# Two-layer S5/attention trunk on one core: S5 constants in portions, no unread products, and a re-ordered first mixer with feature-major queries and keys

## The chip, the core and the metric

The kernel runs on 1 core of a Trainium2 chip. TensorE (PE in the profile, PEld its weight loads), VectorE (DVE), ScalarE (ACT), GpSimd (POOL) and SyncE (SP, which here only issues DMAs) have queues of their own; 16 DMA engines move data. A matmul loads a stationary operand of up to 128 columns and streams the moving operand past it into a PSUM bank. The metric is device time in microseconds; each version is run several times and the median counts.

## What is computed

A trunk of two layers over 256 tokens of 1024 features, float32 in and out. Each layer is half a SwiGLU FFN, a mixer, half a SwiGLU FFN, all with residuals; the first mixer joins an S5 state space model with multi-head latent attention:

```python
def _even_mixer(h, ...):
    u, c_q, c_kv, k_rope = split(h @ w_in, [512, 896, 1152])
    s5_out = _s5(u, ...)                       # diagonal complex states, GELU, gated by a 512x512 product
    q  = rmsnorm(c_q)  @ w_uq                  # 8 heads, 64 plain + 32 rotary
    kv = rmsnorm(c_kv) @ w_ukv                 # 8 heads, 64 key + 64 value
    q_pe, k_pe = rope(q[..., 64:]), rope(k_rope)   # k_pe is shared by the heads
    o = causal_attention([q_nope, q_pe], [k_nope, k_pe], v)
    return concat([s5_out, o]) @ w_out
def reference(x, ...):
    for l in (0, 1):
        x += 0.5 * swiglu(rmsnorm(x)); x += mixer_l(rmsnorm(x)); x += 0.5 * swiglu(rmsnorm(x))
    return rmsnorm(x)
```

The S5 recurrence runs over blocks of four tokens. Powers of the state matrix, the input matrices and the matrices inside a block depend on the weights alone and are made on the chip.

## The kernel before, in words

The tokens are two tiles of 128. Every weight chunk comes by one or two DMAs of 512 KB on SP's queue into one of five stage buffers (`Weights.load`), and `Weights.pre` splits it into a high half (a cast to fp32r by ACT, line 71) and the rest (a subtraction by DVE, line 72). Products with weights are then three fp32r products: high x high, rest x high, high x rest. Transposes, scores, attention values and the S5 products are plain fp32, two passes each except the transposes. The framework orders each engine's queue from the program's order and from its own forecast of when operands are ready; `tc.issue_after(i)` keeps instructions of a block behind instruction `i` on the engine of `i`.

`ffn` loops over 22 blocks of 128 hidden features (`gate_up`, `down`). `begin` norms the residual and makes it feature-major; for the first FFN it also starts the loads and issues 13 small products (`going`, line 262) whose results nothing reads. The first FFN carries `setup()` as a background: after each block, `aside` takes steps of this generator until a budget of 2400 (elements plus 140 for each DVE instruction) is spent; `pause` ends a call at once. `setup` is the rotary tables, a few constants, then `s5_prep`.

`mixer0` runs in this order: the products for cq, ckv, u (`product`, line 771), token-major; `latents` (normed cq and ckv, feature-major); `queries(0)`; u into blocks of four tokens; `keys_values(0)`; `block_inputs` of both halves of the 16 state pairs; `heads_turned`, which transposes queries and keys of each head on PE; then `attend(h)` for eight heads with scores two heads ahead, and between them `states` (DVE multiplications and two scans; half of the read-out on POOL), `outputs` (48 fp32 passes for each half, lines 1030 to 1032), `gelu`, and `glu`; last the output product. `rope` on the queries and the key runs on POOL. At the very end `finish` norms the rows and writes them out.

Of the kernel before, what the change touches and what calls it, by code (L numbers as in the profile page):

```python
# [29 lines left out]
class Weights:  # L30
# [8 lines left out]
    def plan(self, specs):  # L39

        self.specs = list(specs)
        self.pieces = [(i, c) for i, s in enumerate(self.specs) if s is not None
                       for c in range(0, s[0].shape[1], 1024)]

    def load(self, n):
        for i, c in self.pieces[self.loaded:self.loaded + n]:
            ap = self.specs[i][0]
            w = min(1024, ap.shape[1] - c)
# [5 lines left out]
    def pre_in_pieces(self):  # L54
# [14 lines left out]
        for c in range(0, ap.shape[1], 1024):  # L69
            t, w = self.raw.pop(0)  # L70
            nc.scalar.copy(out=hi[:, c:c + w], in_=t[:, :w])  # L71
            nc.vector.tensor_tensor(out=lo[:, c:c + w], in0=t[:, :w], in1=hi[:, c:c + w].bitcast(F32),  # L72
                                    op=ALU.subtract)
            self.load(1)
            yield
# [19 lines left out]
def trunk(ctx: ExitStack, tc: tile.TileContext, x, pos, invf, wff, gains, w_u, w_cq, w_ckv,  # L95
# [72 lines left out]
    def ffn_specs(j):  # L168
# [5 lines left out]
    mix0 = [(w, True) for w in (w_cq[0], w_cq[1], w_ckv[0], w_ckv[1], w_u[0], w_u[1], w_uq[0], w_ukv[0], w_uq[1],  # L174
                                w_ukv[1], w_out0[2], w_glu, w_out0[3], w_out0[0], w_out0[1])]
# [7 lines left out]

    def rsqrt(out, a):

        nc.gpsimd.tensor_tensor(out=out, in0=a, in1=mhalf[:, :a.shape[1]], op=ALU.pow)  # L186
# [48 lines left out]

    def aside(background, quota, last):
# [9 lines left out]
    def begin(prev, row):  # L246
# [5 lines left out]
        if acc is None:  # L252
# [4 lines left out]

            idle = bank("idle")

            def going(n):  # L260
                for _ in range(n):
                    nc.tensor.matmul(idle[:, :128], ident, ident, start=True, stop=True)

            going(4)
# [7 lines left out]
            W.load(STAGED - 2)  # L272
# [6 lines left out]
        if acc is None:  # L279
            pieces = W.pre_in_pieces()  # L280
            ups.append(next(pieces))
            with tc.issue_after(last):
                next(pieces)
            turned_0 = transpose_split(y0, KT, yh, yl, 0)
            going(3)
            with behind_both(turned_0):
                next(pieces)
                r1 = residual(1, acc, factor)
# [5 lines left out]
        y1, last = normed(1, *r1, g)  # L294
# [133 lines left out]
    def sincos(ang, cos, sin, n, tmp):  # L428

        k, kh, r = tmp("k", n), tmp("kh", n), tmp("r", n)  # L430
# [12 lines left out]
        ts(r, r, 3.1415925, -3.1415925, ALU.min, ALU.max)  # L443
        nc.scalar.activation(out=sin, in_=r, func=AF.Sin)
        nc.scalar.activation(out=cos, in_=r, func=AF.Sin, scale=0.5)
        tt(cos, cos, cos, MUL)
# [19 lines left out]

    def cmul_halves(ore, oim, ar, ai, br, bi, t1, t2):
# [13 lines left out]
    ss1 = cst.tile([128, 2, 16], F32, name="ss1")  # L481

# [35 lines left out]
    def rope_tables():  # L518
# [6 lines left out]
        sincos(ang, co, si, 48, lambda n, m: small("rt" + n, m))  # L525
        for t in range(2):
            for (cc, ss, o, h) in ((cc0, ss0, 0, 16), (cc1, ss1, 16, 8)):
# [5 lines left out]
                nc.vector.tensor_copy(out=ss[:, t, h:], in_=s)  # L533

# [29 lines left out]
    def s5_prep():  # L564
# [7 lines left out]
        sc = cst.tile([128, 20, NPAIR], F32, name="s5sc")  # L572
        slots = iter(range(20))
# [17 lines left out]
        dt, mag, ang, co, si = new(), new(), new(), new(), new()  # L591
# [8 lines left out]
        tt(ang, li, dt, MUL)  # L600
        yield
        exp_finish(mag, w, t1, c)
        yield
        sincos(ang, co, si, n, tmp)
        yield

# [4 lines left out]
        cmul(ar[2], ai[2], ar[1], ai[1], ar[1], ai[1], t1, t2)  # L611
        yield
        cmul(ar[3], ai[3], ar[2], ai[2], ar[1], ai[1], t1, t2)
        cmul(ar[4], ai[4], ar[2], ai[2], ar[2], ai[2], t1, t2)
# [10 lines left out]
        cmul(dr, di, co, si, co, si, t1, t2)  # L625
        yield
        er, ei = new(), new()
        cmul(er, ei, dr, di, dr, di, t1, t2)
# [7 lines left out]
        while m < NBLK:  # L636
            nr, ni = (dr, di) if m in (2, 8, 32) else (er, ei)
            orr, oi = (er, ei) if m in (2, 8, 32) else (dr, di)
            cmul(nr, ni, orr, oi, orr, oi, t1, t2)
# [75 lines left out]
        def pause():  # L715
            spent[0] += 1 << 20
            yield

# [5 lines left out]
        yield from pause()  # L724
        for q0 in range(0, NPAIR, 4):
# [745 lines left out]
```

## Time and profile before

| | us |
|---|---|
| median of three runs | 1036.1 |
| the runs | 1036.10, 1028.13, 1036.48 |
| the profiled execution, its span | 1032.36, 1030.5 |
| PE busy | 1003.2 (97%) |
| DVE, ACT, POOL busy | 669.9, 569.1, 50.4 |

Mean granted clock of TensorE over the span: 0.987; 1.00 is 2.4 GHz, 0.50 is 1.2 GHz. An engine's busy time says when instructions of it run; a wait is counted on the engine that stands still and put down to what ended it. A row of the timeline gives start, duration, engine, line, what is written from what, shape and count; merged rows give the time from the first start to the last end.

### The profile page before, as it was taken

The numbers are of one execution on the slowest core, as the hardware profiler recorded it, in microseconds if no ns is written. First come the engines' busy times: TensorE is split into PE (matmuls) and PEld (weight loads), VectorE is DVE, ScalarE is ACT, GpSimd is POOL, SyncE is SP. The second block draws the span as 40 slices with busy tenths as digits, with TensorE's granted clock in tenths as the row PEclk, the third lists the DMA queues.
The fourth block names the chain that finished last, engine by engine and source line by source line (L and its number), as shares of the span: only waits on it lengthen the run. The fifth ranks groups of instructions, "written<-read, shape, count | busy, mean of one in ns | idle before, by whom it ended". The sixth has DMA issues, their size and how long they took to land.

```text
span 1030.5 us, 14762 instructions
## 1 busy us (share of the span) xinstructions
PE 1003.2 (97%) x5540; PEld 861.3 (84%) x5540; DVE 669.9 (65%) x1245; ACT 569.1 (55%) x1030; POOL 50.4 (5%) x81
## 2 busy tenths in 40 slices
PE   8999999989889999999999999999999999999997
PEld 7788899878788888888888888888878887888885
DVE  4889874565867776555558555554657777655543
ACT  5555663666536665555446555553567756555543
POOL 3010000002510000000000000000001100000000
PEclk9999999999969999999999999999999999999999
DMA  8856554316113586555618556553453548656621
GB/s 259 273 153 209 187 187 144 123 46 199 53 42 124 199 291 193 192 188 189 212 56 292 186 191 186 188 192 128 162 165 123 147 137 288 189 192 192 187 80 41
DMA packets 49801, 174.80 MB, mean 170 GB/s; under 512 B 6081, under 2 KB 7105, under 8 KB 49730
## 3 DMA queue, kind: packets, MB, share of 16 engines
q1 hardware_dynamic: 48576, 170.20, 51.0%
q10 hardware_dynamic: 1154, 3.67, 1.1%
q8 instruction: 43, 0.70, 0.3%
q14 instruction: 28, 0.23, 0.1%
HBM read 172.80 MB, written 1.05 MB: 169 GB/s over the span
## 4 chain that ended last, share of the span: by engine, by line
PE 80%; DVE 7%; ACT 4%; DMA 4%; issue 3%; POOL 1%; SPq 0%; POOLq 0%; ACTq 0%; DVEq 0%
PE gu L322 24%; PE acc L355 22%; PE gu L324 12%; PE proj L771 6%; DMA stage<-in_wff_dram 3%; PE acc L782 3%; PE gu L338 2%; DVE wlo L72 2%; PE pu L771 1%; ACT whi L71 1%; PE gt L375 1%; DMA lam<-in_s_lam_dram 1%; PE pt L206 1%; PE ckv L771 1%; PE pz L1063 1%
## 5 line engine op out<-in xcount | busy, mean ns | idle before, releaser
L322 PE MATMUL gu<-y,whi 128*128 128x512 f32 x1216 | 432.6, 398 | 0.0
L72 DVE TENSOR_TENSOR wlo<-stage,whi 128x1024 fp32r<-128x1024 f32 (+1 forms) x236 | 281.2, 1201 | 178.8 <-ACT whi L71 178.5
L324 PE MATMUL gu<-y,wlo 128*128 128x256 f32 x1216 | 341.2, 281 | 0.0
L71 ACT CAST whi<-stage 128x1024 fp32r<-128x1024 f32 (+1 forms) x236 | 240.6, 1033 | 106.7 <-PE gu L322 72.6
L322 PEld LDWEIGHTS gu<-y,whi 128*128 128x128 f32 x1216 | 228.5, 188 | 55.4
L324 PEld LDWEIGHTS gu<-y,wlo 128*128 128x128 f32 x1216 | 229.6, 189 | 2.6
L355 PE MATMUL acc<-dhi,hs 128*128 128x512 f32 x704 | 195.6, 396 | 6.0 <-ACT hs L143 4.6
L355 PEld LDWEIGHTS acc<-dhi,hs 128*128 128x128 f32 x704 | 127.6, 190 | 35.2 <-ACT hs L143 6.0
L72 DVE TENSOR_TENSOR dlo<-stage,dhi 128x1024 fp32r<-128x1024 f32 x88 | 107.1, 1218 | 37.6 <-ACT dhi L71 37.6
L71 ACT CAST dhi<-stage 128x1024 fp32r<-128x1024 f32 x88 | 92.2, 1049 | 44.4 <-DMA stage<-in_wff_dram 44.4
L355 PE MATMUL acc<-dlo,hs 128*128 128x512 f32 x352 | 111.7, 393 | 0.0
L132 DVE TENSOR_TENSOR both<-gu,both 128x256 f32<-128x256 f32 x152 | 63.8, 420 | 55.7 <-ACT both L325 55.4
L325 ACT COPY both<-gu 128x256 f32<-128x256 f32 x152 | 56.0, 369 | 75.8 <-PE gu L324 75.7
L355 PEld LDWEIGHTS acc<-dlo,hs 128*128 128x128 f32 x352 | 67.0, 190 | 14.7
L143 ACT CAST hs<-sh 128x256 fp32r<-128x256 f32 x80 | 32.5, 407 | 71.1 <-DVE sh L132 71.0
L771 PE MATMUL proj<-whi,y 128*128 128x512 f32 x192 | 62.5, 396 | 0.2 <-ACT y L143 0.2
L328 ACT ACTIVATE sh<-both 128x256 f32<-128x256 f32 x76 | 31.8, 419 | 41.7 <-DVE both L132 41.5
L375 PE MATMUL gt<-whi,y 128*128 128x256 f32 x256 | 49.7, 288 | 0.8 <-ACT y L143 0.7
L771 PEld LDWEIGHTS proj<-whi,y 128*128 128x128 f32 x192 | 36.1, 188 | 8.3 <-ACT y L143 0.5
L375 PEld LDWEIGHTS gt<-whi,y 128*128 128x128 f32 x256 | 40.8, 191 | 2.2 <-ACT y L143 2.2
L186 POOL TENSOR_TENSOR rs<-rs,mhalf 128x1 f32<-128x1 f32 x14 | 7.7, 552 | 670.0 <-DVE rs L140 670.0
L132 DVE TENSOR_TENSOR hs<-sh,hs 128x256 fp32r<-128x256 f32 x80 | 33.4, 418 | 7.9 <-ACT hs L143 7.9
(324 smaller groups left out, 1107.1 us busy)
## 6 DMA issues: line engine op xcount, KB each, us to landing
stage<-in_wff_dram SPq DMA_DIRECT2D x264, 512.0 KB, 4.6
stage<-in_w_in_dram SPq DMA_DIRECT2D x24, 512.0 KB, 4.5
stage<-in_w_out_dram SPq DMA_DIRECT2D x16, 512.0 KB, 3.6
gain<-in_gains_dram ACTq DMA_DIRECT2D x6, 512.0 KB, 5.7
stage<-in_w_u_dram SPq DMA_DIRECT2D x4, 512.0 KB, 4.2
xr<-in_x_dram SPq DMA_DIRECT2D x2, 512.0 KB, 5.2
stage<-in_w_cq_dram SPq DMA_DIRECT2D x2, 512.0 KB, 3.8
stage<-in_w_ckv_dram SPq DMA_DIRECT2D x2, 512.0 KB, 4.9
```

Of the source, the lines that this page charges most:

```text
L71: nc.scalar.copy(out=hi[:, c:c + w], in_=t[:, :w])
L72: nc.vector.tensor_tensor(out=lo[:, c:c + w], in0=t[:, :w], in1=hi[:, c:c + w].bitcast(F32), op=ALU.subtract)
L132: return nc.vector.tensor_tensor(out=out, in0=a, in1=b, op=op)
L143: copy = nc.scalar.copy(out=hi, in_=src)
L322: nc.tensor.matmul(gu, gh[:, k, s, :], y2[:, k].rearrange("p s c -> p (s c)"), start=k == 0, stop=False)
L324: nc.tensor.matmul(gu[:, :SEQ], gl[:, k, s, :], yh[:, k, :], start=False, stop=k == KT - 1)
L325: nc.scalar.copy(out=both[:, s], in_=gu[:, SEQ:])
L328: nc.scalar.activation(out=sh[:, 0, :], in_=both[:, 0], func=AF.Silu)
L355: nc.tensor.matmul(acc[t][c], a[:, sl], w[:, c * 512:(c + 1) * 512], start=(f == 0 and n == 0), stop=(f == NF - 1 and n == 2))
L375: last = nc.tensor.matmul(o, a[:, k, sl], w[:, k * 256:(k + 1) * 256], start=(k0 == 0 and n == 0), stop=(k0 > 0 and n == 11))
L771: last = nc.tensor.matmul(acc, a[:, k0 + k, sl], w[:, k * width:(k + 1) * width], start=(k0 == 0 and n == 0), stop=(k0 + per == nk and n = ...
L782: mm = nc.tensor.matmul(acc[t][c], a[:, k0 + k, sl], w[:, o:o + 512], start=(first and k == 0 and n == 0), stop=(last and k == 1 and n == 2))
```

## The change

Early part and first FFN. The 13 unread products go; the second input tile is loaded after one weight piece, not after two. `setup` takes its three generators side by side in three portions, one for each of the first three blocks, behind the last root on POOL (`last_root`), and then runs the rest. Complex squares are made with four instructions in place of six (`csquare`). Every second copy in `within` goes from ACT to DVE.

First mixer. u is projected first, then cq and ckv. Queries and keys are made feature-major directly, with the weights as the stationary operand: each head has 128 rows, 64 plain, 32 rotary and 32 swapped rotary, so that a product with a table (`qtab`) from PSUM does the rotation and the scores' contraction adds both parts; the weight chunk for queries is loaded in pieces of 768 columns and widened from 96 to 128 columns a head while it is split. The shared key part is rotated once on POOL, transposed and copied to all heads. The S5 states are a generator of five steps, all on DVE, taken between other work. Scores run three heads ahead, a head's probabilities are transposed one head ahead, and the first output product is put between heads. `gelu` copies its PSUM bank out first. In `finish` the gain is multiplied in by quarters, and the two scalings and writes are 640 and 384 columns wide.

```diff
 class Weights:
+    def step(spec):
+        return 768 if spec[1] == "queries" else 1024
...
+            if wide == "queries":
+                rows = slice(c // 96, (c + w) // 96)
+                h, l = (a[:, :1536].rearrange("p (r d) -> p r d", d=128)[:, rows] for a in (hi, lo))
+                v = t[:, :w].rearrange("p (r d) -> p r d", d=96)
+                parts = [(h[:, :, :96], l[:, :, :96], v)]
+                parts += [(h[:, :, a:a + 16], l[:, :, a:a + 16], v[:, :, b:b + 16]) for a, b in ((96, 80), (112, 64))]
+            for h, l, v in parts:
+                nc.scalar.copy(out=h, in_=v)
+                nc.vector.tensor_tensor(out=l, in0=v, in1=h.bitcast(F32), op=ALU.subtract)
...
 def begin(prev, row):
-            going(4)
...
-            going(6)
             nc.sync.dma_start(out=xr[0], in_=x[:128])
-            W.load(2)
+            W.load(1)
             nc.sync.dma_start(out=xr[1], in_=x[128:])
...
-            going(3)
...
-        y1, last = normed(1, *r1, g)
+        with behind_both(turned_0):
+            y1, last = normed(1, *r1, g)
...
 def mixer0(prev):
+        cq, ckv = ([bank(n)[:, :w] for _ in range(2)] for n, w in (("cq", 384), ("ckv", 288)))
+        project(cq, 0, 384)
+        u_blocks()
+        project(cq, 1, 384)
+        cqy = [low_rank(cq[t], 384, qg[:, :384]) for t in range(2)]
+        project(ckv, 0, 288)
+        st.append(states(0, *block_inputs(0)))
+        step(0)
+        project(ckv, 1, 288)
+        cky = [low_rank(ckv[t][:, :256], 256, qg[:, 384:]) for t in range(2)]
+        kd = key_rotation()
...
+        step(0)
+        st.append(states(1, *block_inputs(1)))
...
 def queries(g):
+            for b in range(2):
+                pq = bank("pq").rearrange("p (h c) -> p h c", h=2)
+                for j in range(2):
+                    for n, (k, w, a) in enumerate(highs_first(range(3), wh, wl, cqh, cql)):
+                        nc.tensor.matmul(pq[:, j], w[:, k, 2 * b + j], a[:, k, :], start=n == 0, stop=n == 8)
+                h = 4 * g + 2 * b
+                tt(qT[:, h:h + 2, :], pq, qtab.unsqueeze(1).to_broadcast([128, 2, SEQ]), MUL)
...
 def states(b, v_re, v_im):
+            for z, x, y, op in ((z_re, v_re, v_im, ADD), (z_im, v_im, v_re, SUB)):
+                tt(z, x, c, MUL)
+                tt(t1, y, s, MUL)
+                tt(z, z, t1, op)
+                yield
             scan(z_re)
             scan(z_im)
             yield
...
-            for out, x, y, op in ((xs_im[:, h, o], z_re[:, :, a], s[:, :, a], MUL), (t2, z_im[:, :, a], c[:, :, a], MUL),
-                                  (xs_im[:, h, o], xs_im[:, h, o], t2, ADD)):
-                nc.gpsimd.tensor_tensor(out=out, in0=x, in1=y, op=op)
+            for xs, x, y, op in ((xs_re, z_re, z_im, SUB), (xs_im, z_im, z_re, ADD)):
+                tt(xs[:, h, o], x[:, :, a], c[:, :, a], MUL)
+                tt(t1, y[:, :, a], s[:, :, a], MUL)
+                tt(xs[:, h, o], xs[:, h, o], t1, op)
+                yield
...
+        queries(0)
...
+        step(1)
+        keys(0)
+        step(0)
+        key_values(0)
+        for h in range(3):
+            sc[h] = scores(h)
+        step(1)
+        step(0)
         queries(1)
+        step(0)
+        sc[0] = turned(sc[0], pb)
         attend(0)
+        step(1)
+        keys(1)
+        key_values(1)
         attend(1)
+        step(1)
         yp = outputs(0)
         attend(2)
+        step(1)
         attend(3)
         osb = normalised(0)
+        g0 = gelu(yp)
         yp = outputs(1)
         heads_out(0, osb)
+        attend(4)
...
 def setup():
-        rope_tables()
-        yield from mixer_constants()
-        yield from s5_prep()
+        parts = [mixer_constants(), s5_prep(), rope_tables()]
+        for _ in range(3):
+            with tc.issue_after(last_root[0]):
+                for part in parts:
+                    next(part, None)
+            yield from pause()
+        for part in parts[:0:-1]:
+            yield from part
```

## Rows read from the trace of the kernel before

**Rows 1.** Windows: stretch, length, busy of PE, PEld, DVE, ACT, POOL; PEclk, DMA, GB/s.

```profile
0.00:12.10 12.10, 10.64 (x39) 7.87 (x39) 3.43 (x6) 4.64 (x8) 5.48 (x16) 1.00 0.85 310
12.10:48.60 36.50, 32.59 (x200) 28.46 (x199) 28.18 (x51) 23.42 (x35) 3.43 (x2) 0.95 0.82 253
48.60:210.70 162.10, 162.10 (x953) 142.35 (x951) 119.01 (x288) 94.95 (x159) 6.54 (x5) 1.00 0.53 165
210.70:220.60 9.90, 7.23 (x25) 5.50 (x25) 5.99 (x11) 4.32 (x11) 0.56 (x1) 0.83 0.26 96
220.60:344.50 123.90, 115.23 (x686) 103.39 (x687) 87.65 (x172) 64.84 (x145) 23.88 (x40) 0.93 0.32 108
281.00:287.00 6.00, 0.59 (x4) 0.46 (x4) 6.00 (x9) 0.03 (x1) 3.66 (x3) 0.79 0.00 0
287.00:301.30 14.30, 14.30 (x65) 13.83 (x66) 8.25 (x18) 3.94 (x8) 0.77 (x1) 0.50 0.24 74
```

**Rows 2.** Waits of PE: line, cause: total us, times, longest us.

```profile
PE yp L1031 <- DVE xs_re L132: 5.4, 1, 5.4
PE acc L355 <- ACT hs L143: 4.6, 3, 2.3
PE pt L206 <- DVE y L136: 2.5, 5, 1.2
PE po L1003 <- ACT pT L804: 1.5, 2, 0.9
```

**Rows 3.** Timeline of the start: start us, us, engine, line, operation.

```profile
6.60 1.43 DVE L136 SCALAR_TENSOR_TENSOR y<-xr,rs,g 128x512 f32<-128x512 f32 x2 [0.74 <-POOL rs L186]
...
7.17 2.93 PE L262 MATMUL idle<-ident 128*128 128x128 f32 x12
...
9.90 1.77 PE L206 MATMUL pt<-ident,y 128*128 128x128 f32 x8
...
11.51 0.83 PE L262 MATMUL idle<-ident 128*128 128x128 f32 x6
...
13.08 2.91 POOL L453 TENSOR_TENSOR s5w<-euler,lam 128x16 f32<-128x16 f32 x1 [4.65 <-DMA lam<-in_s_lam_dram]
...
17.34 0.66 PE L206 MATMUL pt<-ident,y 128*128 128x128 f32 x4 [1.20 <-DVE y L136]
```

**Rows 4.** Timeline of PE, rows of equal products, on the high clock.

```profile
223.44 1.03 PE L771 MATMUL cq<-whi,y 128*128 128x384 f32 x5
...
242.79 1.07 PE L771 MATMUL pu<-whi,y 128*128 128x512 f32 x4
...
250.60 0.34 PE L771 MATMUL pq<-whi,cqh 128*128 128x384 f32 x1
...
261.81 0.61 PE L926 MATMUL v_im<-u,e_im 128*128 128x64 f32 x4
...
265.36 0.60 PE L974 MATMUL pt<-ident,q_sb 128*96 128x128 f32 x4
...
346.84 0.76 PE L375 MATMUL gt<-whi,y 128*128 128x256 f32 x5
```

**Rows 5.** Timeline of PE in outputs(0), on the low clock.

```profile
287.63 0.64 PE L1030 MATMUL yp<-u,tmat 128*128 128x64 f32 x2
```

**Rows 6.** Groups, DVE, 220.6 to 344.5: count | busy us, mean ns | idle before.

```profile
L72 DVE TENSOR_TENSOR wlo<-stage,whi 128x1024 fp32r<-128x1024 f32 x22 | 26.3, 1219 | 8.8 <-ACT whi L71 8.8
...
L937 DVE TENSOR_TENSOR_SCAN z_im<-mag,z_im 128x512 f32<-128x512 f32 x2 | 3.4, 1698 | 0.0
L789 DVE CUSTOM_DVE_ANT_0 s<-sp,mask 128x256 f32<-128x256 f32 x8 | 3.3, 414 | 0.0
...
L937 DVE TENSOR_TENSOR_SCAN z_re<-mag,z_re 128x512 f32<-128x512 f32 x2 | 2.4, 1211 | 0.0
...
L132 DVE TENSOR_TENSOR z_re<-v_re,cosn 128x512 f32<-128x512 f32 x2 | 1.4, 684 | 2.9 <-PE v_re L925 2.9
```

**Rows 7.** Tile xs_re: count, duration min/median/max ns, first and last start.

```profile
L132 DVE TENSOR_TENSOR xs_re<-xs_re,t x2: 668/1180/1691, 285.0 to 291.2; 128x504 f32<-128x504 f32 x2
```

**Rows 8.** Timeline of DVE in the last norm.

```profile
1024.61 0.69 DVE L132 TENSOR_TENSOR yo<-xr,gain 128x512 f32<-128x512 f32 x1
```

More of the change, by code (lines that the diff above doesn't have):

```diff
@@ L533, in rope_tables, with rotation_table @@
                 nc.vector.tensor_copy(out=ss[:, t, h:], in_=s)
+        nc.gpsimd.memset(ct[:, :, :64], 1.0)
+        nc.vector.tensor_copy(out=ct[:, :, 64:96], in_=cc0)
+        nc.vector.tensor_copy(out=ct[:, :, 96:], in_=ss0)
+    def rotation_table():
+        pt = bank("pt")[:, :SEQ]
+        for t in range(2):
+            nc.tensor.transpose(pt[:, t * 128:(t + 1) * 128], ct[:, t], ident)
+        nc.scalar.copy(out=qtab, in_=pt)
     def rope(v, nh, cc, ss, half, eng=None):
@@ L773, in product, with out_product @@
         return last.ins
-    def out_product(acc, t, ws, hi, lo, k0, first, last):
+    def out_product(acc, t, ws, hi, lo, k0, first, last, ks=(0, 1)):
         wh, wl = ws
         sl = slice(t * 128, (t + 1) * 128)
-        for k in range(2):
+        for k in ks:
             for n, (w, a) in enumerate(three(wh, wl, hi, lo)):
@@ new lines, in queries, with keys @@
+            for b in range(2):
[5 more added lines that the diff above has]
+                tt(qT[:, h:h + 2, :], pq, qtab.unsqueeze(1).to_broadcast([128, 2, SEQ]), MUL)
+            more()
+        def keys(g):
+            wh, wl = (w[:, :1024].rearrange("p (k s c) -> p k s c", k=2, s=2) for w in queue[0])
+            pk = bank("pk").rearrange("p (j c) -> p j c", j=2)
+            for j in range(2):
+                for n, (k, w, a) in enumerate(highs_first(range(2), wh, wl, ckh, ckl)):
+                    nc.tensor.matmul(pk[:, j], w[:, k, 0, 128 * j:128 * j + 128], a[:, k, :], start=n == 0,
+                                     stop=n == 5)
+            for r in range(2):
+                nc.scalar.copy(out=kT[:64, 4 * g + r:4 * g + 4:2, :], in_=pk[64 * r:64 * r + 64])
@@ new lines, in key_values @@
+        def key_values(g):
+            wh, wl = (w[:, :1024].rearrange("p (k s c) -> p k s c", k=2, s=2) for w in queue.pop(0))
+            pv = bank("pv").rearrange("p (t c) -> p t c", t=2)
+            for t in range(2):
+                sl = slice(t * 128, (t + 1) * 128)
+                for n, (k, w, a) in enumerate(highs_first(range(2), wh, wl, ckh, ckl)):
+                    nc.tensor.matmul(pv[:, t], a[:, k, sl], w[:, k, 1, :], start=n == 0, stop=n == 5)
+            nc.scalar.copy(out=v_sb[:, :, 256 * g:256 * g + 256], in_=pv)
+            more()
@@ L994, in scores, with values @@
             return s
[L996 removed]
+        def values(h, pT):
             g, k = divmod(h, 4)
@@ L1082, in attend @@
             values(h, sc.pop(h))
-        heads_turned(0)
-        sc = {0: scores(0), 1: scores(1)}
-        next(st[0])
+        queries(0)
+        pt = bank("pt")[:, :SEQ]
+        for t in range(2):
+            nc.tensor.transpose(pt[:, t * 128:(t + 1) * 128], kd[:, t], ident)
+        for g in range(2):
+            nc.scalar.copy(out=kT[64:, 4 * g:4 * g + 4, :], in_=pt[64:].unsqueeze(1).to_broadcast([64, 4, SEQ]))
+        step(1)
+        keys(0)
+        step(0)
+        key_values(0)
```

306 lines of the change are left out of this document (137 added, 169 removed).

## The prediction

> **What bounds the kernel now.** I read the busy time by stages first. From 48.6 to 210.7 us TensorE (PE) is busy all the time at full granted clock [rows 1], so there a shorter VectorE (DVE) or ScalarE (ACT) step is worth nothing; the reader should look for the stages where PE is not full. There are three, and the change touches each. The start (0 to 48.6) has 1.5 + 3.9 us without PE work. The end of the first FFN (210.7 to 220.6) has 2.7 us idle and a mean clock of 0.83. The first mixer (220.6 to 344.5) has 123.9 - 115.2 = 8.7 us idle, and its stretch from 287.0 to 301.3 ran at granted clock 0.50, the 1.2 GHz level, all through: 14.3 / 2 = 7.15 us lost. Next the waits of PE by cause [rows 2]: the longest, 5.4 us, is that of `outputs(0)` for `xs_re`, the S5 states, which DVE makes; in the six microseconds around it DVE is busy 6.00 of 6.00 and PE 0.59 [rows 1]. The clock fell in that wait and came back only after the 48 small products of `outputs(0)` and some of the attention. So the mixer's chain is DVE's S5 states, then a cold PE.
>
> **The sum** is made against the profiled execution: 1032.4 us, of which 1030.5 is the span. It lies 3.7 us under the median of the three runs (1036.1), inside their spread of 8.3.
>
> **Prices of PE work.** A single 384-column product lasts 0.34 us, five in a row 1.03, so one more costs (1.03 - 0.34) / 4 = 0.17 and 0.17 is the tail. In the same way 512 columns cost (1.07 - 0.17) / 4 = 0.225, 256 columns 0.12, a 64-column fp32 pass or a transpose 0.11 [rows 4]. A small fp32 product is two passes, 0.22. On the low clock two passes take (0.64 - 0.21) = 0.43, that is 0.215 each [rows 5].
>
> **The start.** The 13 unread products (26 passes) go. Twelve of those passes hold PE from 7.17 to 10.1, though the normed rows of tile 0 began to come at 6.60 + 0.7 = 7.3; their transposes start at 9.90 [rows 3]: 2.5 us gained. The S5 power `s5w` (2.91 us on GpSimd, POOL) runs ahead of the root of tile 1, which makes PE wait 1.20 us [rows 3]; the new order puts all POOL work of the first three portions behind that root: 1.2 gained. Against it stands the clock. A single pass lasts 0.17 + 0.11 = 0.28; the first twelve unread ones stand (2.93 - 0.28) / 11 = 0.24 apart, the last six (0.83 - 0.28) / 5 = 0.11 [rows 3]: PE was on the low level at 7.2 and on the high one by 11.5, after those twelve passes and eight transposes. Now the eight transposes and about twelve real products of 24 must stand in for them, at 0.24 instead of 0.12: 1.4 lost. Take 2.5 + 1.2 - 1.4 = 2.3 us gained. Bounds: 6.2 gained if the 3.9 us of waits behind it go too; 2.9 lost if all 24 products run slow and the transfers, whose share is already 0.82 there [rows 1], set the pace anyway. The swap of one weight piece and the second input tile on SP's queue, and the portions' DMAs, which are the same seven on the same queue, lie inside these bounds.
>
> The Trainium skill says that PE's default state is throttled and that activity releases it (TensorE: Matmul & The Clock Gate, "What's actually happening"). It speaks against removing the unread products, and the spacing 0.24 then 0.11 agrees [rows 3]; by it alone the start would be the cold rival below.
>
> **S5's early work.** The squares in place of general complex products save two DVE instructions in each of nine places, under a PE that is full. Counting the budget of 2400 through both generators, the transposes of w are reached after thirteen calls of `aside` before and after (three fixed portions, then as many as before), so the last copies still fall on the last two blocks of the FFN. There six of ten `tmat` copies go from ACT to DVE, and the first two mixer chunks are wider by a quarter. PE's longest wait for `hs` is 2.3 us, in that place [rows 2]. ACT is freed by about what DVE gains, and `hs` needs both: I take 0. Bounds: the wait and the slow clock go, 2.3 + 0.17 x 9.9 = 4.0 gained; DVE's extra copies and wider rests come first, 1.5 lost.
>
> **The first mixer, PE work.** Queries: 36 products of 384 columns (6.1) become 72 of 256 (8.6): +2.5. Keys and values: 24 of 512 (5.4) become 48 of 256 (5.8): +0.4. The 32 transposes of heads go, two for the keys and two for the query table come: -28 x 0.11 = -3.1. Together -0.2. Scores contract over 128 rows in place of 96 and cost the same columns. u first moves products, no more.
>
> **The first mixer, DVE work.** The three POOL instructions of each half of `xs_im` go to DVE: 6 x 0.68 = 4.1 more. Four head copies go and four products by the query table come, of one size. Beside POOL the same DVE instruction took up to 1691 ns against 668 [rows 7], and the scans of `z_im` a mean of 1698 against 1211 for `z_re` [rows 6]: two and two such pairs give about 2 us back, and with the other stretched ones more. The DVE sum hardly changes; what changes is when it can start, for u is there 25 us earlier against the rest.
>
> So does DVE reach `xs` before PE reaches `outputs(0)`? From the end of the first block inputs PE has: second half of ckv 24 x 0.13 (288 columns, between the prices of 256 and 384), ten transposes, 32 passes of block inputs, 72 + 48 products of 256 columns, five scores at 0.66 (two passes of 128 columns and two of 256, these at double price), two heads' transposes and values: 3.1 + 1.1 + 3.5 + 14.4 + 3.3 + 2.1, with seams 28. DVE has, by [rows 6]: half 0 of the states 12 x 0.68 + 2 x 1.21 = 10.6; weight rests of five chunks, 2 x 1.22 + 2 x 2.2 + 2.4 = 9.2 (the query chunk in three parts is an estimate from 1.22 for 1024 elements plus small ones); latents 2.9; query tables 2.7; row maxima of five heads 5.0. That is 30.4: 2.4 us late. With the first two parts of half 1, which stand ahead in the code, 34.5: 6.4 late. Starts overlap a little, so I take 4 us of waits, spread over scores, turned heads and outputs. Bounds: 0 (the order lets half 0 through and overlap hides the rest) and 12.9 (all 10.6 of half 1 first).
>
> Mixer: -8.7 idle, -7.15 slow clock, -0.2 work, +4.0 new waits: -12.0; bounds -16.0 and, with the clock lost as before, about 0. This takes it that no one wait cools PE: waits of 0.9 and 1.2 us stand in [rows 2], and the slow stretch came only behind the 5.4.
>
> **The last norm.** The multiplication by the gain (0.69 us for 512 columns [rows 8]) is cut in quarters and put between the residuals, and the scaling is split 640 to 384 to level DVE and ACT: 0.7 gained at most, 0 at least; I take 0.4.
>
> Sum: -2.3 + 0 - 12.0 - 0.4 = -14.7; 1032.4 - 14.7 = **1017.7 us**.
>
> **Rivals.**
> *DVE late, PE cold* (0.22). One wait before `outputs(0)` of 6.4, 2.4 more than taken, and the clock falls as it did before: 48 x 0.105 = 5.0 in `outputs(0)` and about 2 behind: 1017.7 + 9.4 = 1027.1. For it: DVE's sum is above PE's by my own count. Against: the three-heads lead gives PE other work.
> *Cold start* (0.08). No gain from the first transposes, all 24 products slow: 1017.7 + 2.3 + 2.9 = 1022.9. For it: the two spacings in [rows 3].
> *Nothing moved* (0.10). The S5 chain and the weight rests keep DVE the bound, so 8.7 us of idle and 7.15 of slow clock come back at another place and the start is paced by DMA: 1017.7 + 4.7 + 7.15 + 2.3 = 1031.9. It would show DVE full wherever PE waits.
> *Slower* (0.07). A wait at the first scores, for the keys that go through ACT, POOL, a transpose and ACT again, cools PE, and it stays at 1.2 GHz through the attention, as it stayed 14.3 us through full work [rows 1]: about 230 passes at +0.105 (24), 60 products at +0.12 (7), the wait 3: 1017.7 + 34 = 1052. It decides if PE stands at the first scores about as long as it stood at `outputs(0)`. Against: POOL has nothing else to do then, and the second queries can be put before.
>
> **How the numbers follow.** The forecast has the rest, 0.53, with its own range 1008 to 1025. I call a change of over 1%, 10.4 us, what can be told from none. Faster: 0.53 + 0.08 and nearly half of the first rival, 0.71. Within 1%: the rest of it and "nothing moved", 0.22. Slower: 0.07. The range, 1005 to 1033, leaves out the slow rival, some of "nothing moved" and a mixer with no wait at all plus the best start.
>
> **What would show it.** In the changed profile: PE's transposes of tile 0 near 7.5 us and no 1.2 us wait for tile 1; the first 256-column products 0.24 apart and later ones 0.12; no POOL work between the latents' roots and the end of the mixer but the key rotation; no clock of 0.50 behind 265; the mixer some 112 us long; `glu` near 310 less the start's gain. A wait of PE for `xs` with DVE full on the left of it, or a stretch at 0.50 in `outputs`, means the first rival. I am wrong altogether if the mixer's PE idle time is not below 6 us.

## The result

| | us |
|---|---|
| before, median of four runs | 1036.3 (1028.1 to 1037.9) |
| after, median of four runs | 1021.2 (1018.1 to 1022.1) |
| ratio, 95% interval | 0.9858, 0.9814 to 0.9901 |
| spans of the two profiled executions | 1030.5 and 1020.3 |

The kernel is faster by 15.1 us; 14.7 was forecast, 1017.7 predicted, range 1005 to 1033. The two profiles differ by 10.2 us only: the profiled execution of before had a mean granted clock of 0.987, while of the 13 runs of that kernel beside e9 to e11 ten had 0.977 to 0.982 and 1034 to 1040 us, and three had 0.987 to 0.989 and 1027 to 1030. So the sums of steps below are made against 10.2, and the forecast is nearer to the median than its steps deserve.

Stages, cut at PE's transposes of the normed rows of tile 0 (first FFN, first mixer, second FFN), from the timelines of PE, with the medians of all kernels that were run:

| kernel | median us | first FFN begins | its length | mixer | rest |
|---|---|---|---|---|---|
| before | 1036.3 | 9.90 | 210.7 | 123.9 | 686.0 |
| after | 1021.2 | 7.59 | 205.2 | 122.4 | 685.1 |
| e1, unread products back | 1023.3 | 9.90 | 204.9 | 122.6 | 685.6 |
| e2, portions undone | 1018.7 | 7.58 | 204.1 | 117.4 | 686.0 |
| e3, block inputs first | 1013.9 | 7.51 | 205.6 | 114.1 | 685.6 |
| e4, mixer undone | 1026.0 | 7.54 | 203.9 | 129.2 | 687.9 |
| e5, order of the start undone | 1022.8 | 7.46 | 205.8 | 121.3 | 685.1 |
| e6, unread products in the wait | 1016.7 | 7.51 | 205.2 | 116.7 | 684.8 |
| e7, e3 and relief ahead of the gate | 1012.8 | 7.42 | 205.3 | 109.8 | 686.0 |
| e8, e7 and portions undone | 1009.8 | 7.63 | 203.7 | 109.7 | 685.7 |
| e9, e2 and e5 | 1023.1 | 7.63 | 207.2 | 120.3 | 685.3 |
| e10, start undone in full | 1025.5 | 9.90 | 205.2 | 121.6 | 684.8 |
| e11, e8 and read-out on POOL | 1008.2 | 7.60 | 204.1 | 110.0 | 684.9 |
| e12, squares and copies undone | 1021.6 | 7.55 | 207.4 | 122.8 | 685.1 |

Medians are over four runs (ten for e10) that lie 2 to 5 us apart, 7 for e10, 10 for before and 12 for e4; stage lengths are of one execution each. The kernels were timed in five groups, with a median of before from 1036.3 to 1038.3, so 2 us between kernels of different groups cannot be told from none by the medians alone.

Windows of after, where [rows 1] has those of before (stretch, length, busy time of PE, PEld, DVE, ACT, POOL, then PEclk, DMA share, GB/s; a clock between 0.50 and 1.00 is the mean of a stretch that holds both levels):

```profile
212.81:217.40 4.59, 4.56 (x16) 3.42 (x17) 3.09 (x6) 2.66 (x4) 0.56 (x1) 0.63 0.00 0
247.79:250.79 3.00, 0.00 (x0) 0.00 (x1) 2.74 (x6) 0.89 (x5) 0.55 (x1) 1.00 0.13 22
250.79:261.50 10.71, 10.71 (x53) 10.71 (x54) 5.39 (x9) 0.81 (x3) 1.73 (x5) 0.53 0.12 44
306.80:308.70 1.90, 0.01 (x1) 0.01 (x1) 1.82 (x7) 0.43 (x1) 0.00 (x0) 1.00 0.00 0
308.70:316.20 7.50, 6.98 (x32) 6.41 (x33) 4.36 (x5) 3.46 (x5) 0.00 (x0) 0.55 0.39 117
212.81:335.21 122.40, 114.94 (x717) 105.24 (x718) 84.42 (x183) 64.88 (x145) 5.20 (x12) 0.92 0.31 102
```

Waits of PE in the mixer of after, 212.8 to 335.2 (line, cause: total us, times, longest), beside [rows 2]:

```profile
PE pt L221 <- DVE cy L148: 3.0, 1, 3.0
PE pt L1068 <- DVE osb L144: 1.9, 1, 1.9
PE pt L221 <- DVE y L148: 1.8, 1, 1.8
PE sp L1035 <- ACT qk L947: 1.1, 1, 1.1
PE po L1050 <- ACT pT L845: 0.8, 1, 0.8
PE pz L1113 <- DVE gl L144: 0.5, 1, 0.5
```

The wait of 5.4 us for `xs_re` and the slow stretch of 14.3 us behind it are gone. In their place stand two waits that the kernel before did not have, 3.0 for the second latent and 1.9 for the normed heads, each with a slow stretch behind it: 10.71 us at 0.53 and 7.50 at 0.55. With 4.59 at 0.63 at the mixer's begin they cost 5.0 + 3.4 + 1.7 = 10.1 us, more than the 7.15 of the old one. (The mean clock of 0.93 over 123.9 us would give 8.7 for before, but 0.21 x 6.00 = 1.3 of that lies in the wait itself [rows 1], where PE had no work to slow down.) Idle time of PE fell from 8.7 to 122.40 - 114.94 = 7.5.

With POOL idle, DVE's read-out no longer stretches, where [rows 7] had up to 1691 ns (instructions of the mixer of after by line and form; busy us, mean ns, then idle time before):

```profile
L144 DVE TENSOR_TENSOR xs_re<-z_re,cosn 128x504 f32<-128x504 f32 x2 | 1.4, 718 | 0.0
```

**Why the second latent was late.** DVE in after, start, duration, operation:

```profile
245.84 0.15 DVE L152 TENSOR_SCALAR ss<-ss 128x1 f32<-128x1 f32 x1 [0.35 <-ACT cy L205]
...
246.73 0.48 DVE L148 SCALAR_TENSOR_TENSOR cy<-ckv,rs,qg 128x256 f32<-128x256 f32 x1
247.13 1.22 DVE L980 TENSOR_TENSOR_SCAN z_re<-mag,z_re 128x512 f32<-128x512 f32 x1
248.26 1.20 DVE L85 TENSOR_TENSOR wlo<-stage,whi 128x1024 fp32r<-128x1024 f32 x1
249.37 0.15 DVE L152 TENSOR_SCALAR ss<-ss 128x1 f32<-128x1 f32 x1
250.25 0.48 DVE L148 SCALAR_TENSOR_TENSOR cy<-ckv,rs,qg 128x256 f32<-128x256 f32 x1 [0.26 <-POOL rs L201]
```

and PE and ACT beside it:

```profile
246.73 1.04 PE L221 MATMUL pt<-ident,cy 128*128 128x128 f32 x8
250.79 0.44 PE L221 MATMUL pt<-ident,cy 128*128 128x128 f32 x2 [3.02 <-DVE cy L148]
...
251.47 0.64 PE L968 MATMUL v_re<-u,e_re 128*128 128x64 f32 x2
```

```profile
247.63 0.19 ACT L205 ACTIVATION_READ_ACCUMULATOR cy<-ckv 128x1 f32 x1
```

The sum of squares of tile 1 was complete on ACT at 247.82; the 0.15 us instruction that needs it stood behind a scan of the S5 states and a weight rest until 249.37. That is some 1.5 of the 3.0 us; the rest is the chain itself, from the sum to the root on POOL and the scaling. No run moved that instruction, so its share is read from the rows and not tested. PE's next work, the block inputs of the second half (32 passes), needed only `u`, ready some ten microseconds before, but stood behind the latent's transposes in PE's queue.

### The profile page after: what moved, and what is told of

Same layout as the page of the kernel before. It is cut to its first block, busy times and chain, and to the rows that moved or that the text cites. A ratio compares the mean times of both kernels' runs of the same rounds, so it can differ in the third digit from the quotient of the medians.

```text
span 1020.3 us, 14761 instructions
## 1 busy us (share of the span) xinstructions
PE 995.2 (98%) x5546; PEld 857.3 (84%) x5546; DVE 670.3 (66%) x1251; ACT 567.5 (56%) x1027; POOL 34.3 (3%) x56
## 4 chain that ended last, share of the span: by engine, by line
PE 86%; DVE 6%; ACT 3%; DMA 2%; issue 2%; POOL 1%; SPq 0%; POOLq 0%; DVEq 0%; ACTq 0%
PE gu L333 26%; PE acc L366 22%; PE gu L335 13%; PE proj L812 6%; PE acc L823 2%; PE gu L349 2%; PE gt L386 2%; DVE wlo L85 2%; DMA stage<-in_wff_dram 2%; PE pu L812 1%; PE pq L934 1%; PE pz L1113 1%; PE cq L812 1%; PE pt L221 1%; ACT whi L84 1%
## 5 line engine op out<-in xcount | busy, mean ns | idle before, releaser
L85 DVE TENSOR_TENSOR wlo<-stage,whi 128x1024 fp32r<-128x1024 f32 (+3 forms) x244 | 282.4, 1169 | 185.0 <-ACT whi L84 184.7
L84 ACT CAST whi<-stage 128x1024 fp32r<-128x1024 f32 (+3 forms) x244 | 242.2, 1008 | 119.9 <-PE gu L333 73.3
L366 PE MATMUL acc<-dhi,hs 128*128 128x512 f32 x704 | 192.7, 392 | 2.0 <-ACT hs L155 1.5
L366 PEld LDWEIGHTS acc<-dlo,hs 128*128 128x128 f32 x352 | 66.1, 188 | 14.3
L812 PE MATMUL proj<-wlo,y 128*128 128x512 f32 x96 | 37.5, 391 | 0.0
```

Source lines behind the costliest of these rows:

```text
L84: nc.scalar.copy(out=h, in_=v)
L85: nc.vector.tensor_tensor(out=l, in0=v, in1=h.bitcast(F32), op=ALU.subtract)
L366: nc.tensor.matmul(acc[t][c], a[:, sl], w[:, c * 512:(c + 1) * 512], start=(f == 0 and n == 0), stop=(f == NF - 1 and n == 2))
L812: last = nc.tensor.matmul(acc, a[:, k0 + k, sl], w[:, k * width:(k + 1) * width], start=(k0 == 0 and n == 0), stop=(k0 + per == nk and n = ...
```

## The experiments

**e1: the unread products back**, at their three places.

```diff
+            going(4)
             g = [bank("g") for _ in range(2)]
...
+            going(6)
             nc.sync.dma_start(out=xr[0], in_=x[:128])
...
             turned_0 = transpose_split(y0, KT, yh, yl, 0)
+            going(3)
```

> The changed kernel with the 13 unread products of the start put back at their three places (4, 6 and 3 of them); nothing else. Theory, the unread products stood in the way: the transposes of tile 0 go back from 7.59 us to near 9.9 and the first real product from 9.93 to near 12, 2.1 later; the first eight real products, which stood 0.21 apart, then come at 0.12, 0.8 back: slower by 1 to 2, some 1022.5. Rival one, the transfers set the pace of the start: the later begin is caught up by 20 us, no change. Rival two, a warm PE is worth more than the early begin: faster by 1 to 2.

1023.3, 2.2 slower; the two profiled executions, both at a mean clock of 0.988, differ by 2.6. Tile 0's transposes went back to 9.90 and the first real product to 12.08; the first FFN kept its length (204.9), so nothing was caught up. The warm PE gave back 0.2 us by tile 1's transposes, 1.9 later (eight products at 0.12 in place of 0.21, less a wait of 0.7 for a weight rest). The theory holds, though the price of the cold begin is smaller than I wrote. The granted clock of the profile reads 1.00 here in both kernels; the low level shows only in the spacing, 0.21 against 0.12. Start of after and of e1:

```profile
7.59 1.97 PE L221 MATMUL pt<-ident,y 128*128 128x128 f32 x8 [0.55 <-DVE y L148]
9.93 0.58 PE L386 MATMUL gt<-whi,y 128*128 128x256 f32 x1 [0.38 <-ACT y L155]
...
11.80 1.07 PE L386 MATMUL gt<-whi,y 128*128 128x256 f32 x5
...
14.04 1.09 PE L221 MATMUL pt<-ident,y 128*128 128x128 f32 x8
```

```profile
9.90 1.75 PE L221 MATMUL pt<-ident,y 128*128 128x128 f32 x8
...
12.08 0.36 PE L395 MATMUL gt<-whi,y 128*128 128x256 f32 x1
...
15.95 1.03 PE L221 MATMUL pt<-ident,y 128*128 128x128 f32 x8
```

**e2, e5, e9, e10: portions and order.** e2 undoes the portions, e5 the order inside the start; e9 does both, and e10 brings back the unread products too.

```diff
 e2:
-        parts = [mixer_constants(), s5_prep(), rope_tables()]
-        for _ in range(3):
...
+        for _ in rope_tables():
+            pass
+        yield from mixer_constants()
+        yield from s5_prep()
 e5:
-            W.load(1)
+            W.load(2)
             nc.sync.dma_start(out=xr[1], in_=x[128:])
...
                 next(pieces)
-                r1 = residual(1, acc, factor)
             turned_0 = transpose_split(y0, KT, yh, yl, 0)
             with behind_both(turned_0):
                 next(pieces)
+                r1 = residual(1, acc, factor)
...
-        with behind_both(turned_0):
-            y1, last = normed(1, *r1, g)
+        y1, last = normed(1, *r1, g)
```

> The changed kernel, but the S5 constants come in the order of before (rotary tables, then the constants, then the powers, one after another) and not in three portions side by side behind the root. Theory, the portions took DVE and POOL out of the way of the first blocks: the waits of PE between 15 and 45 us (1.2 for the normed rows of tile 1, 1.6 and 0.4 for hs) and the slow clock behind them come back, 5 to 6 us, some 1026.5. Rival, these waits vanished with the earlier start and the other order of the two loads: no more than 1 us, some 1021.5.

> The changed kernel with the order of before inside the start: two weight pieces ahead of the second input tile, and the residual and the norm of tile 1 at their old places; the unread products stay out. Theory, this order is what removed the waits of 15 to 45 us (with tile 1 early, ACT widens the weight pieces earlier, their buffers come free and the next transfers start earlier): a wait for the normed rows of tile 1 and one for hs near 40 come back with a slow stretch, the first FFN is 3 to 5 us longer, some 1025. Rival, the fewer DVE instructions of the S5 constants removed them: no change, some 1021.

> The changed kernel with both the order of before inside the start and the S5 constants one after another; the unread products stay out. Each of the two alone left the first FFN at 204 to 206 us from the first transposes. Theory, each covers for the other (the portions keep the S5 power off POOL until the root of tile 1 is through, and the early residual has the root ready before that power comes): with both undone the 1.2 us wait for the normed rows of tile 1 and one for hs near 37 come back and that length is 208 to 210; 1022 to 1025. Rival, what made it shorter is in neither (fewer DVE instructions, half of the copies on DVE): 204 to 206 again, some 1019 to 1021.

> The changed kernel with the start of before in full: the 13 unread products, the order and the S5 constants one after another. What is left of the change outside the mixer are the complex squares, the copies on DVE and the last norm. Theory, the parts add up: the first transposes at 9.9, the first FFN 208 to 210.7 long as before, and the mixer as in the changed kernel, 1026 to 1029. Rival, the squares and copies shortened the first FFN: 205, 1022 to 1024.

e2: 1018.7. The theory falls, the waits do not come back; without the portions the kernel was even 2.4 us faster, though the ranges overlap (1016.8 to 1019.5, 1018.1 to 1022.1). Its mixer, 5.0 shorter than in after, is that of an execution at full clock at the mixer's begin and at the heads, and its two slower runs have a clock of 0.989, as after has; what the portions cost is not settled. e5: 1022.8, no wait for tile 1 either, the first FFN 0.6 longer. e9: 1023.1, first FFN 207.2: now the wait is there, and POOL shows why:

```profile
12.49 2.91 POOL L468 TENSOR_TENSOR s5w<-euler,lam 128x16 f32<-128x16 f32 x1 [2.09 <-DMA lam<-in_s_lam_dram]
15.37 0.55 POOL L201 TENSOR_TENSOR rs<-rs,mhalf 128x1 f32<-128x1 f32 x1
```

```profile
16.76 0.66 PE L221 MATMUL pt<-ident,y 128*128 128x128 f32 x4 [2.71 <-DVE y L148]
```

The root of tile 1 stands 2.9 us behind the S5 power, as in the kernel before. Either edit alone prevents it, by the portions' `issue_after` or by the early residual; in these runs having both adds nothing. e10: 1025.5, so the start in full is worth some 4.3 us. Its first FFN is 205.2 long, not 208 to 210: the theory that the start's edits made the whole difference to 210.7 falls.

**e12: squares and copies undone.** `csquare` calls `cmul` with six instructions, and in `within`:

```diff
-                if i % 2:
-                    nc.vector.tensor_copy(out=dst, in_=src)
-                else:
-                    nc.scalar.copy(out=dst, in_=src)
+                nc.scalar.copy(out=dst, in_=src)
```

> The changed kernel with the complex squares made by six instructions again and all copies of the block matrices on ACT, as before; start and mixer stay changed. Theory, these two edits took work out of the way of hs: the wait for hs at the end of the first FFN grows from 1.5 to 2.3 us and one near 40 us comes back, the stretch from the first transposes to the mixer's is 207 to 209 in place of 205.2, some 1024. Rival, they lie under a full PE: 205, some 1021. The first FFN of the kernel before, 210.7 long, is then put down to waits that differ from one execution to the next.

1021.6, no difference that can be told, though the first FFN of this execution was 2.2 us longer. Not `hs` was late (1.4 us, as in after) but the normed rows of tile 0, 3.92 us in place of 1.75, for ACT had the copies and casts ahead of its squares:

```profile
207.94 0.62 ACT L790 COPY tmat<-dd 32x512 f32<-32x512 f32 x1
208.59 2.00 ACT L84 CAST whi<-stage 128x1024 fp32r<-128x1024 f32 x2
...
211.77 0.63 ACT L230 ACTIVATE y<-xr 128x512 f32<-128x512 f32 x1
```

In after the first of these squares starts at 209.66. No single edit brings back the 210.7 of before. Nearest to its start is e10, which waits for `hs` in the same place, 0.80 and 0.42 in place of 1.60 and 0.42, but at full clock, where before had 0.78 from 40.68 to 48.57 (1.7 us); and it has no wait for `hs` at the end of the FFN, where before has 2.3 and a clock of 0.83. Which edit, or which chance, makes that difference is open.

**e4: the mixer undone.** The functions `mixer0`, `mix0` and what they call are those of before; start, first FFN and last norm stay changed.

> The changed kernel with the first mixer of before (its order, its token-major queries and keys, its read-out on POOL, its weight pieces); the start, the first FFN and the last norm as changed. By the two traces the start and the first FFN give 7.8, the last norm and the rest 0.9 and the mixer 1.5. Theory, the traces stand for the medians: 1022 to 1024, and the new mixer is worth 1 to 2. Rival, the profiled execution of before had a better mixer than the median one (its 1032.4 against 1036.3): 1027 to 1029, and the new mixer is worth 6 or more.

1026.0, between the two expectations, with runs at 1021.1, 1021.6, 1030.4 and 1032.7 and clocks of 0.989, 0.989, 0.982 and 0.978. The wait of 5.4 for `xs_re` was there again; in the profiled execution, the third, PE then ran at 0.54 from 276.9 to 297.0, at 0.96 for two microseconds, and at 0.51 again from 299.1 to 309.3, with no wait in between but one of 0.6 at 296.3:

```profile
297.05 0.39 PE L1059 MATMUL yp<-u,tmat 128*128 128x64 f32 x2
...
299.14 0.64 PE L1059 MATMUL yp<-u,tmat 128*128 128x64 f32 x2
```

The old mixer is one wait with slow stretches of varying length behind it; against such runs the new one is worth 4.9 us in the median, against the profile of before 1.5.

**e3: block inputs first.**

```diff
+        st.append(states(1, *block_inputs(1)))
         for t in range(2):
             transpose_split(cky[t], 2, ckh, ckl, t)
         step(0)
-        st.append(states(1, *block_inputs(1)))
```

> The changed kernel with the block inputs of the second half of the states (32 passes, 3.5 us) put ahead of the four transposes of the second latent, for which PE stood still 3.02 us. Theory, that one wait cost the mixer itself and 10 us at the low clock: the wait goes below 0.5, no stretch at 0.50 stands behind 251, and the mixer is 8 us shorter: some 1013. Rival, DVE is the bound of the mixer: the wait comes back before the scores or before the first outputs, with DVE full there, and no more than 2 us are gained, some 1020.

1013.9, 7.3 faster than after, the mixer 8.4 shorter. The 32 passes run from 246.55 to 250.07 and the transposes follow without a wait, at full clock:

```profile
250.07 0.61 PE L221 MATMUL pt<-ident,cy 128*128 128x128 f32 x4
```

Up to the first outputs DVE shows up as a wait of 0.7 for `xs_im` and nowhere else: the theory holds, the rival falls. The wait of 1.9 at the normed heads stays, with 0.62 from 300 to 306 behind it.

**e6: unread products in the wait**, the order otherwise as in after.

```diff
+        idle = bank("idle")
+        for _ in range(13):
+            nc.tensor.matmul(idle[:, :128], ident, ident, start=True, stop=True)
         for t in range(2):
             transpose_split(cky[t], 2, ckh, ckl, t)
```

> The changed kernel with 13 small products that nothing reads put on PE just ahead of the four transposes of the second latent, where PE stood still for 3.02 us; they fill the wait and do no work. Theory, most of the loss there is the clock that the wait brings down: the transposes start when they did, but no stretch at 0.50 follows, and the mixer is some 5 us shorter, 1016. Rival one, the clock falls for another reason: no change, 1021. Rival two, the work behind is bound by DVE: the slow stretch goes, but PE then waits as long before the scores, 1020 to 1021.

1016.7, 4.5 faster, the mixer 5.7 shorter. Windows of e6 at the filler and behind it:

```profile
247.35:250.26 2.91, 2.91 (x29) 2.91 (x27) 2.64 (x5) 1.28 (x6) 0.55 (x1) 1.00 0.02 8
250.26:255.00 4.74, 4.53 (x41) 4.32 (x40) 3.87 (x8) 0.83 (x3) 1.74 (x5) 1.00 0.31 114
```

The time of the wait is spent as before, on nothing; the clock stays at 1.00 (in after 0.53, to 261.5). From the first transposes of the latents to those of the last normed heads PE takes 61.96 us in after, 57.13 in e6 and 54.72 in e3. So this one wait with its slow stretch cost 7.2 us, of which 4.8 are clock and 2.4 the wait. The other 1.1 of e3's 8.4 is the mixer's begin, which ran at full clock in that execution, and the other 1.0 of e6's 5.7 is a shorter slow stretch at the gate; neither follows from the edit. The same trick cost 2.2 us at the start, where it stood in front of real work, and gave 4.5 here, where PE had none.

**e7, e8: relief ahead of the gate product.** e7 is e3 with

```diff
-                        nc.vector.tensor_scalar_mul(dst, src, 0.5)
+                        (nc.gpsimd if i == 2 else nc.vector).tensor_scalar_mul(dst, src, 0.5)
...
+        halves(gh[:, :2], gl[:, :2], gt[:, :2])
         attended(w2, 1, 0, True, (0,))
         in_channels(1, g1)
         attend(7)
-        halves(gh, gl, gt)
-        attended(w2, 1, 0, True, (1,))
         osb = normalised(1)
+        halves(gh[:, 2:], gl[:, 2:], gt[:, 2:])
+        attended(w2, 1, 0, True, (1,))
         heads_out(1, osb)
```

and e8 is e7 without the portions.

> The block inputs ahead of the second latent's transposes as in the run with that edit alone (1013.9), and besides relief for DVE ahead of the gate product: a quarter of the copies into channels goes to POOL, the first half of the gate's operand is split early, and the normed heads are scaled ahead of the second half. Theory, DVE's chain there makes PE wait (1.9 for the heads, 0.6 for the gate's rests) and cools it: the waits fall below 1.2 together, the slow stretch behind goes (3.7 us), 1009 to 1010. Rival, DVE is full there in any order: the waits stay near 2.5 and the clock falls all the same, 1013 to 1014.

> The kernel with both edits of the mixer (block inputs first, relief ahead of the gate product) and the S5 constants in the order of before. Theory, the three effects stand in different stages and add up: 1013.9 less 4 for the gate and less 1.5 to 2.5 for the portions, 1007 to 1009. Rival, the portions' 2.5 lay in a slow stretch at 212 to 217 that does not come in every execution: no gain from them here, 1010.

In after DVE made the heads wait like this:

```profile
304.77 3.40 DVE L1100 TENSOR_SCALAR gt<-gq 32x128 f32<-32x128 f32 x12
308.21 0.76 DVE L144 TENSOR_TENSOR osb<-po,r 128x256 f32<-128x256 f32 x2
```

e7: 1012.8, with two runs at 1010.2 and 1010.7 and two near 1015. In its profile (1010.7) the two waits are 0.8 and none (0.4 for the gate's sigmoid is new), the clock does not fall and the mixer is 4.3 shorter than in e3. In the median only 1.1 is left of that, so the gain of the relief is not settled; the clocks of the two runs near 1015, 0.992 against 0.998, suggest that they still had a slow stretch, and no profile shows where. e8: 1009.8 (1008.2 to 1011.7), where 1007 to 1009 was expected and the rival, no gain from the portions, had 1010: that the three effects add up is not shown. The kernel is faster than both, with a ratio to before of 0.9744 (0.9701 to 0.9786).

**e11: the read-out on POOL.** In e8, for each half, as in the kernel before:

```diff
+            for out, x, y, op in ((xs_im[:, h, o], z_re[:, :, a], s[:, :, a], MUL), (t2, z_im[:, :, a], c[:, :, a], MUL),
+                                  (xs_im[:, h, o], xs_im[:, h, o], t2, ADD)):
+                nc.gpsimd.tensor_tensor(out=out, in0=x, in1=y, op=op)
```

> The kernel of the combined run (1009.8) with one part of the change undone: the three instructions of each half that make the imaginary states go back to POOL. Theory, POOL takes 1.25 to 1.58 us for each and DVE's instructions beside it stretch: the imaginary states of half 0 come 4 us late, PE waits 2 to 4 us for them before the first outputs, and the clock falls behind that wait, as in the kernel before; 1014 to 1018. Rival, DVE was the bound and has 4.1 us less to do: no wait, 1008 to 1010.

1008.2 (1007.3 to 1009.6): no slower. My theory falls; there is no wait for `xs`. POOL is slow and DVE stretches beside it, but both have time:

```profile
271.20 2.16 POOL L999 TENSOR_TENSOR xs_im<-z_re,sinn 128x504 f32<-128x504 f32 x1 [9.81 <-DVE mx L1044]
273.32 1.70 POOL L999 TENSOR_TENSOR t<-z_im,cosn 128x504 f32<-128x504 f32 x1
```

```profile
272.23 1.67 DVE L144 TENSOR_TENSOR xs_re<-z_re,cosn 128x504 f32<-128x504 f32 x1
273.82 2.28 DVE L85 TENSOR_TENSOR wlo<-stage,whi 128x1024 fp32r<-128x1024 f32 x1
...
278.89 0.67 DVE L144 TENSOR_TENSOR xs_re<-xs_re,t 128x504 f32<-128x504 f32 x1
```

Beside POOL a DVE instruction of 0.68 us takes 1.67 and one of 1.22 takes 2.28. The Trainium skill says that a DVE instruction with two SBUF inputs contends with a GpSimd instruction that reads SBUF (SBUF — State Buffer, "Who interferes with whom"); these rows agree. In e8 the two engines' work is DVE 82.8 and POOL 10.8 us in the mixer, in e11 82.9 and 21.4: what DVE hands over it loses again to the stretching, so moving the read-out was worth nothing in either direction.

## Why the prediction came out as it did, step by step

**The start: forecast -2.3, measured -7.2 by the end of the first `down` products.** The parts that were costed came near: transposes 2.3 earlier (2.5 forecast); tile 1 without its wait; eight slow products 0.21 apart, not twelve at 0.24, so 0.8 lost where 1.4 was put, and e1 found the warm PE worth 0.2 net. What the sum left to the bounds is the larger half: PE's transposes of tile 1 are 3.3 us earlier, the first `down` products 4.9 (35.83 for 40.68) and the next gate products 7.2 (41.34 for 48.57). Windows of after (PE alone, PEclk, DMA share, GB/s):

```profile
7.59:35.83 28.24, 27.80 (x180) 1.00 0.90 302
35.83:41.34 5.51, 5.51 (x27) 1.00 0.94 357
```

The same two stretches of before, up to the first `down` products and through them:

```profile
9.90:40.68 30.78, 27.29 (x188) 1.00 0.82 254
40.68:48.57 7.89, 7.47 (x25) 0.78 0.86 265
```

I had put the 3.9 us of waits behind the start as a bound, and the slow clock behind them nowhere. (The bound of 6.2 also counts the wait of 1.2 for tile 1 twice, as it is one of the 3.9; it should have been 5.0.) Some 1.8 us of slow clock (0.05 x 36.5) were to be read in the window that stood at 0.95 [rows 1].

**The end of the first FFN: forecast 0, measured -0.6.** The wait for `hs` fell from 2.31 to 1.48, but that for the normed rows rose from 0.38 to 1.75: a PE at full clock is through tile 1's products sooner and stands before the same norm chain. The wait for `hs` goes with the portions: without them (e2, e8 to e11) it is gone, and in e2, e8 and e11 the first FFN is 1.1 to 1.5 shorter. But e4, with the portions and a wait of 1.5 there, has 203.9 too, so what they cost is not shown.

**The mixer: forecast -12.0, measured -1.5.** This is the step that failed, and the sentence of it is "This takes it that no one wait cools PE". By the terms of the sum: idle time -8.7 plus 4.0 new waits, measured -1.2, for 7.5 of idle are left; slow clock -7.15, measured 10.1 in place of 7.15, so +2.9; PE work -0.2, measured about -3.2 at full clock (114.94 - 10.1 against 115.23 - 7.15; e8's mixer, at a clock of 1.00, has 105.7); together -1.5. So the idle time came out 3.5 us above the forecast, the clock behind them, 10.1 us, was taken as nothing, and 2 to 3 us of less PE work, which the count of products did not have and no run explains, came to its help. The reason given for the clock, that a slow stretch came only behind the wait of 5.4, did not hold in its own rows: [rows 1] has 0.83 from 210.7 to 220.6 and 0.95 from 12.1 to 48.6, where the waits are 2.3 us and less. I looked for DVE's lateness at `outputs(0)`, where the old wait stood, and counted what DVE has to do up to there; I did not ask which 0.15 us instruction stands behind a scan in DVE's queue while PE has only its product to do. By my own condition (idle time below 6 us) I was wrong altogether: it is 7.5. The sign "no clock of 0.50 behind 265" failed too, with 0.55 from 308.7. e3, with one of the two waits gone, has a mixer of 114.1 us, and e7, with both relieved, one of 109.8, where 112 was forecast.

**DVE late at the outputs: 30.4 or 34.5 against 28.** Up to `outputs(0)` DVE is not late: after shows no wait for `xs`, and with PE 8 us sooner there (e3) it is 0.7. As a wait for the outputs the 4 us taken were too much; the count left out that DVE works on half 0 while PE still has the products of ckv and the latents. The 4.1 us of read-out are no term at all (e11).

**The last norm: forecast -0.4, measured +0.7.** From PE's last product to the end of the span: 7.14 us before, 7.87 after. The gains in quarters of the other tile stand on DVE between the last product and the residual of tile 1:

```profile
1012.04 0.39 PE L366 MATMUL acc<-dlo,hs 128*128 128x512 f32 x1
```

```profile
1012.10 0.55 DVE L1454 TENSOR_SCALAR yo<-yo,rs 128x640 f32<-128x640 f32 x1 [0.33 <-POOL rs L201]
1012.57 0.75 DVE L144 TENSOR_TENSOR yo<-xr,gain 128x256 f32<-128x256 f32 x2
1013.24 0.75 DVE L148 SCALAR_TENSOR_TENSOR xr<-acc,xr 128x256 f32<-128x256 f32 x2
1013.91 0.75 DVE L144 TENSOR_TENSOR yo<-xr,gain 128x256 f32<-128x256 f32 x2
...
1015.64 0.55 DVE L1454 TENSOR_SCALAR yo<-yo,rs 128x640 f32<-128x640 f32 x1 [0.66 <-POOL rs L201]
```

The residual of tile 1 starts 0.81 us after PE's last product and started 0.47 after it before. The other half of the 0.7 lies at the last write: from the end of DVE's scaling to the end of the span 4.1 us in place of 3.8, with 320 KB in SP's write in place of 256. The FFNs and the second mixer in between were 1.6 shorter, which no step had; as this rest lies between 684.8 and 687.9 us in the other runs, it may be chance.

**The rivals.** "DVE late, PE cold" was right in kind and wrong in place: PE cooled behind a DVE wait, at the latent and at the heads. "Cold start" did not happen. The first scores waited 1.1 us for the keys, and that wait cooled nothing. What the Trainium skill says of a throttled default state that activity releases (TensorE: Matmul & The Clock Gate, "What's actually happening"), which spoke against removing the unread products, was true of the clock (products 0.21 apart until 11.8) and small in time (e1). "Nothing moved", at 0.10, is what the mixer did by itself: 7.5 us of idle time and 10.1 of slow clock at other places, with DVE busy for 2.74 of 3.00 and 1.82 of 1.90 us while PE waited. Its reason, DVE as the bound, falls with e3, and its other half, a start paced by the transfers, did not happen.

**Why the number was near all the same.** Start 4.9 better, first FFN's end 0.6 better, mixer 10.5 worse, last norm and rest 0.5 better: -10.2 by the profiles. That these misses, and then the medians, brought it back to 0.4 of the forecast is luck. The medians add 4.9: the profiled execution of before lies 3.9 under its median, that of after 0.9 over its own. Most runs of before have a lower clock than its profile: (1 - 0.979) x 1036 = 22 us lost to the clock against (1 - 0.988) x 1021 = 12 after, an estimate from the granted clocks of the runs, and 13 in the profiled execution of before. Undone one at a time, the new mixer is worth 4.9 us (e4), the start 4.3 (e10) and the squares and copies nothing that can be told (e12): some 9 of the 15.1. No run places the rest.

## What to carry to other kernels

When a wait of a busy PE goes, look for the next wait in the new order, in the queue of every engine that feeds PE, and price it with the slow clock behind it: here 3.0 us of waiting cost 7.2. Put products that need nothing new ahead of the transposes that wait; where there are none, products that nobody reads are worth having inside such a wait (e6), and not in front of real work (e1). A profile shows one execution: compare its granted clock with that of the timed runs before summing against it.

## What the runs showed of the hardware

The same waits did not always bring the clock down. In after a wait of 1.48 and one of 1.75 us stand 5 us apart ahead of the mixer and PE ran slow behind them, in e3 waits of 1.9 and 1.77 in the same place, and it did not (in after the same stretch of the mixer stands above at 0.63):

```profile
213.12:217.70 4.58, 4.53 (x23) 3.32 (x24) 3.14 (x6) 2.66 (x4) 0.56 (x1) 1.00 0.00 0
```

At the normed heads e2 waited 1.93 and 0.76 at full clock where after waited 1.92 and 0.52 and fell to 0.55:

```profile
304.00:311.00 7.00, 5.44 (x39) 4.79 (x40) 5.13 (x8) 4.29 (x6) 0.00 (x0) 1.00 0.29 83
```

So in these executions waits of some 2 us cost either themselves alone or 1.7 to 3.4 us of slow clock besides, and runs of one kernel differ by as much (e8: 1008.2 at 0.999, 1011.7 at 0.994). What decides is open. The Trainium skill says that the number of products at the low clock at a kernel's start differs from run to run (TensorE: Matmul & The Clock Gate, "What's actually happening"); the rows here show a like difference behind waits inside the kernel.
